# A diffusion layer on one Trainium2 core: the DRAM additions of the halves of `w_down` in quarters, one transfer to a channel of the up stage

## The chip, the cores and the metric

The kernel runs on one core of a Trainium2 chip. A core has five engines with a queue each: TensorE (PE) for matrix products, VectorE (DVE), ScalarE (ACT) and GpSimd (POOL) for work on elements, and SyncE (SP), which here only issues DMAs. The weight loads of PE are shown on their own as PEld. Sixteen DMA engines move data between DRAM and the on-chip memory, and from DRAM to DRAM. A DMA is issued by an instruction in some engine's queue: SP's and POOL's are the ones that matter here.

The metric is the device time of one execution in microseconds (us). The time before is 1707.95 us, the median of three runs (1703.12 to 1720.14).

## The reference

One layer of a bidirectional hybrid backbone: a mixer of two groups of gated linear recurrences (GLA and HGRN2), then a convolutional feed-forward block, both modulated by a conditioning vector. There are 128 context tokens and 1024 latent tokens (a grid of 16 rows of 64), and the model width is 1024. The change touches the feed-forward block alone:

```python
def conv_ffn(h, w_up, conv_w, conv_b, w_down, grid):
    u = dw_conv(h @ w_up, conv_w, conv_b, grid)     # w_up: 1024 x 5632; 3x3 depthwise conv
    gate, up = jnp.split(u, 2, axis=-1)             # 2816 hidden channels each
    return (jax.nn.silu(gate) * up) @ w_down        # w_down: 2816 x 1024

def trunk_layer(x, mod, ...):
    ...
    h = rmsnorm(x, norm2) * (1 + scale2) + shift2
    x = x + gate2 * conv_ffn(h, w_ffn_up, ffn_conv, b_ffn_conv, w_ffn_down, grid)
```

Everything is in float32. The outputs are the two token blocks after a last RMSNorm, and the new recurrence states of the context.

## The kernel before, in words

**Products.** A float32 operand is split into a high part (a copy in the matrix format, on ACT) and a low part (the difference, `split_lo`, L62, on POOL or DVE), and a product is three matrix products of such parts. The two large products of the feed-forward block are done with seven block products in place of eight, which needs sums of blocks of both operands.

**The up stage** is a loop over 22 channels (L1531); a channel is 128 gate columns and the 128 up columns that go with them. For each channel PE does seven products of 12 matrix multiplications each (`up`, L1457), the same columns for the 128 context tokens (`up_prompt`), and two transposes (`prompt_columns`, L1507). The transposes come once per channel and so mark PE's place. DVE and ACT do the convolutions out of PSUM (`conv_rows`, `conv_prompt`).

**The weights of a channel** come in two rows, row 1 for the gate columns and row 2 for the up columns. `load_row` (L1284) loads a row in two halves of 256 KB into the tile `ra`, issued by SP; each moves 512 runs of 512 bytes to 128 partitions. `weight_sums` (L1305) makes four block sums out of both rows on POOL: first s1 = row-2 block 1 + row-2 block 2 (L1307), then s2 (L1308), s4 (L1309) and s3 (L1310), in the tile `sr`. `split_slots` (L1292) makes the high and low parts for PE (`wuh` on ACT, `wul` on POOL). Rows are fetched ahead: in iteration c of the loop the rows of channel c+2 are loaded as soon as the splits and sums of channel c+1 have freed their part of `ra`. Row 2 is issued first; L1307 is the first instruction that needs it.

**The second half of a channel** (`second_half`, L1515) runs one iteration later: the rest of the convolution, the product of the gated halves on POOL (L1522), the store of the result to the DRAM tile `scr_g` (L1523, issued by POOL), one transfer out of `sums_todo` if any is left (channels 1 and up; issued by POOL right behind L1522), and in odd channels the sums over tokens (`token_sums`, L1384, four POOL instructions and a store to `scr_s`).

**The down stage** also uses seven products, over 11 pairs of channels, with the operands read back from DRAM. Four of its weight operands are sums of blocks of `w_down`; they are made in DRAM, in the four tiles `scr_t` of 11 x 128 x 512 floats (2,816 KB each), by the transfers of `sums_todo`. `halves[h][f]` is a view of `w_down`: 11 blocks of 128 rows that lie 256 rows apart, 512 of the 1024 columns. In `scr_t` the same 1,408 rows lie one behind the other. A transfer with `accum_op=ALU.add` adds its source to what the destination holds; the others copy. The eight transfers go out with channels 1 to 8. The sums are read in the third, fifth, sixth and seventh of the down stage's eight products. Its first weights are fetched by SP during the last channels, from `scr_g` and `w_down`.

**What sets the order.** PE's products of the up stage are chained by hand (`chained`, L1449); the rest is placed by a scheduler at build time, in each engine's one in-order queue. The transfers of `sums_todo` are tied to follow L1522 of their channel. POOL's DMAs all go through one queue (q0 in the profile), SP's through another (q1).

Of the kernel before, what the change touches and what calls it, by code (L numbers as in the profile page):

```python
# [13 lines left out]
ALU = mybir.AluOpType  # L14
# [11 lines left out]
NPAIR = 11  # L26
# [20 lines left out]
def kernel(ctx: ExitStack, tc: tile.TileContext, ins, outs, stop=None):  # L47
    nc = tc.nc
# [40 lines left out]
    scr_t = [dram.tile([NPAIR, P, 512], F32, name=f"scr_t{i}") for i in range(4)]  # L89
# [1294 lines left out]
    def token_sums(j):  # L1384
# [8 lines left out]
        nc.gpsimd.dma_start(scr_s[j], t)  # L1393


    halves = [
        [w_down.rearrange("(j h p) f -> h j p f", h=2, p=P)[h][:, :, fs] for fs in (lo_f, hi_f)] for h in range(2)
    ]
    sums_todo = [
        lambda: nc.gpsimd.dma_start(scr_t[0], halves[0][1]),  # L1400
        lambda: nc.gpsimd.dma_start(scr_t[2], halves[1][1]),
        lambda: nc.gpsimd.dma_start(scr_t[0], halves[0][0], accum_op=ALU.add),
        lambda: nc.gpsimd.dma_start(scr_t[2], halves[0][1], accum_op=ALU.add),
        lambda: nc.gpsimd.dma_start(scr_t[1], scr_t[0]),
        lambda: nc.gpsimd.dma_start(scr_t[1], halves[1][1], accum_op=ALU.add),
        lambda: nc.gpsimd.dma_start(scr_t[3], scr_t[1]),
        lambda: nc.gpsimd.dma_start(scr_t[3], halves[1][0], accum_op=ALU.add),
    ]

    def conv_rows(u, ch, acc, ra=0, rb=NROW):  # L1410

# [393 lines left out]
def build(nc, shapes, outs_kind="ExternalOutput", stop=None):  # L1805
    ins = {
        n: nc.dram_tensor(f"in_{n}_dram", s, dt, kind="ExternalInput").ap() for n, (s, dt) in shapes.items()
    }
    outs = [
        nc.dram_tensor(f"out_{i}_dram", s, F32, kind="ExternalOutput").ap() for i, (s, _) in enumerate(_OUTS)  # L1810
    ]
    with tile.TileContext(nc, schedule_with_timeline_sim=True) as tc:
        kernel(tc, ins, outs, stop)
# [14 lines left out]
```

## Time and profile before

| | |
|---|---|
| median of three runs | 1707.95 us (1703.12 to 1720.14) |
| profiled execution: its own time | 1704.19 us |
| its span, first to last instruction | 1702.4 us |
| granted clock of PE over the span | 0.972 |
| PE busy | 1599.4 us (94%) |
| DVE busy | 1189.7 us (70%) |
| ACT busy | 752.5 us (44%) |
| POOL busy | 712.5 us (42%) |
| up stage, first to last transposes of PE | 921 to 1438 us |
| down stage | from about 1440 us to the end |

Busy times are shares of the whole span and say nothing of a single stage. In the lists quoted below, a row of a timeline has the start in us, the duration in us, the engine, the line, the operation, output and input by the program's names; in brackets the idle time of the engine just before it and what ended it. A row of DMA issues has the number of issues, the size of one, and the median time from issue to landing. A row of stretches has the stretch, its length, then for each engine the busy time and the count of instructions, the granted clock, the mean busy share of the 16 DMA engines, and GB/s read and written together.

### The profile page before, as it was taken

What the parts mean: (1) busy time and instruction counts of PE and PEld (TensorE: products, weight loads), DVE (VectorE), ACT (ScalarE), POOL (GpSimd) and SP (SyncE); (2) the same over time, 40 slices, a digit from 0 to 9 for tenths busy, and PEclk for the clock granted to TensorE, in tenths of its full rate; (3) what the DMA queues carried; (4) which work ended last, traced back from release to release, by engine and by line L of the source; (5) the groups of instructions that cost most, each with busy time, mean ns of one, the idle gap of its engine ahead of it and who ended that gap; (6) DMA issues with size and microseconds to landing.
All of it is one profiled execution on the core that took longest, in us unless ns stands there. A gap on an engine that the chain in (4) does not pass through costs nothing.

```text
span 1702.4 us, 23982 instructions
## 1 busy us (share of the span) xinstructions
PE 1599.4 (94%) x9050; PEld 1346.1 (79%) x9050; DVE 1189.7 (70%) x1720; ACT 752.5 (44%) x1397; POOL 712.5 (42%) x523
## 2 busy tenths in 40 slices
PE   7999998999999999899877998789999999999997
PEld 2788886998999999878656887567788887788886
DVE  4554456066576667854669997678899999777665
ACT  4443345253545344511664443333444444447444
POOL 2402012232423323111255987777999997300001
PEclk9999999999999999999978999899899999999999
DMA  9234343221322304253821357676222224679862
GB/s 353 78 95 124 116 132 106 74 90 50 111 64 69 115 32 157 77 230 139 306 99 38 115 183 170 190 188 157 98 94 102 96 97 147 253 259 338 284 193 117
DMA packets 166349, 244.18 MB, mean 143 GB/s; under 512 B 14132, under 2 KB 110626, under 8 KB 164186
## 3 DMA queue, kind: packets, MB, share of 16 engines
q1 hardware_dynamic: 142583, 168.54, 30.8%
q0 software_dynamic: 23040, 73.43, 13.1%
q8 instruction: 71, 1.16, 0.3%
q10 hardware_dynamic: 611, 0.68, 0.1%
q14 instruction: 44, 0.36, 0.1%
HBM read 186.95 MB, written 78.71 MB: 156 GB/s over the span
## 4 chain that ended last, share of the span: by engine, by line
PE 73%; DMA 9%; POOL 6%; DVE 6%; issue 4%; ACT 1%; SPq 0%; POOLq 0%; DVEq 0%; ACTq 0%
PE u L1316 16%; PE mm L580 15%; PE mm L594 6%; PE lv L862 5%; PE xb L1690 5%; PE yb L1690 5%; DMA ra<-in_w_ffn_up_dram 5%; PE mm L720 3%; PE x L1490 3%; POOL wul L62 2%; PE yb L1741 2%; PE u L1211 2%; PE mm L485 1%; PE x L903 1%; PE o L938 1%
## 5 line engine op out<-in xcount | busy, mean ns | idle before, releaser
L1426 DVE SCALAR_TENSOR_TENSOR acc<-u,convc,acc 128x945 f32<-128x945 f32 (+2 forms) x352 | 426.8, 1218 | 10.8 <-ACT acc L1414 4.4
L62 POOL TENSOR_TENSOR wl<-raw,wh 128x1024 fp32r<-128x1024 f32 x42 | 102.1, 2435 | 271.8 <-ACT wh L123 246.9
L580 PE MATMUL mm<-h1h,wh 128*128 128x384 f32 x528 | 184.7, 350 | 0.0
L580 PE MATMUL mm<-h1l,wh 128*128 128x384 f32 x528 | 180.9, 343 | 0.0
L580 PE MATMUL mm<-h1h,wl 128*128 128x384 f32 x528 | 180.9, 343 | 0.0
L862 PE MATMUL lv<-Q,m 64*128 64x128 f32 (+1 forms) x1008 | 126.6, 295 | 12.5 <-DVE Q L871 6.7
L879 DVE COPY_PREDICATED S<-masks,lv 128x384 f32<-128x384 uint8 x168 | 98.7, 587 | 54.5 <-PE lv L862 54.3
L62 POOL TENSOR_TENSOR wul<-sr,wuh 128x512 fp32r<-128x512 f32 (+1 forms) x68 | 121.9, 1793 | 33.5 <-ACT wuh L1302 33.1
L855 ACT ACTIVATE m<-k 128x384 f32<-128x384 f32 x126 | 69.8, 556 | 142.3 <-DVE k L873 119.2
L871 DVE TENSOR_TENSOR Q<-Q,fb 128x384 f32<-128x384 f32 x126 | 92.8, 736 | 54.7 <-PE lv L862 54.0
L862 PEld LDWEIGHTS lv<-Q,m 64*128 64x128 f32 (+1 forms) x1008 | 107.5, 190 | 26.6 <-issue 10.7
L62 POOL TENSOR_TENSOR wul<-ra,wuh 128x1024 fp32r<-128x1024 f32 x46 | 116.6, 2535 | 11.8 <-ACT wuh L1302 7.6
L580 PEld LDWEIGHTS mm<-h1h,wh 128*128 128x128 f32 x528 | 100.3, 190 | 5.5 <-issue 3.7
L580 PEld LDWEIGHTS mm<-h1l,wh 128*128 128x128 f32 x528 | 100.1, 190 | 1.5 <-issue 0.8
L1665 POOL TENSOR_TENSOR sq<-sq,mhalf 128x1 f32<-128x1 f32 x9 | 11.1, 1237 | 214.1 <-DVE sq L1662 214.1
L580 PEld LDWEIGHTS mm<-h1h,wl 128*128 128x128 f32 x528 | 99.9, 189 | 0.7 <-issue 0.6
L123 ACT ACTIVATE wh<-raw 128x1024 fp32r<-128x1024 f32 x55 | 58.1, 1058 | 62.3 <-DMA raw<-in_w_in_dram 22.8
L594 PE MATMUL mm<-wh,h1h 128*128 128x256 f32 x288 | 83.2, 289 | 0.0
L594 PE MATMUL mm<-wl,h1h 128*128 128x256 f32 x288 | 80.9, 281 | 0.0
L873 DVE TENSOR_TENSOR k<-k,fb 128x384 f32<-128x384 f32 x126 | 76.1, 608 | 6.7 <-ACT m L855 2.7
L594 PE MATMUL mm<-wh,h1l 128*128 128x256 f32 x288 | 80.8, 281 | 0.0
L1302 ACT ACTIVATE wuh<-ra 128x1024 fp32r<-128x1024 f32 x44 | 46.3, 1053 | 62.0 <-DMA ra<-in_w_ffn_up_dram 27.4
(346 smaller groups left out, 4478.9 us busy)
## 6 DMA issues: line engine op xcount, KB each, us to landing
ra<-in_w_ffn_up_dram SPq DMA_DIRECT2D x88, 256.0 KB, 3.1
scr_t<-in_w_ffn_down_dram POOLq DMA_DIRECT2D x6, 2816.0 KB, 27.0
raw<-in_w_in_dram SPq DMA_DIRECT2D x32, 512.0 KB, 4.5
raw<-in_w_ada_dram SPq DMA_DIRECT2D x32, 512.0 KB, 3.7
scr_g<-acc POOLq DMA_DIRECT2D x22, 576.0 KB, 4.0
scr_s<-late POOLq DMA_DIRECT2D x11, 1024.0 KB, 5.0
wa<-in_w_ada_dram SPq DMA_DIRECT2D x16, 512.0 KB, 6.1
raw<-in_w_out_dram SPq DMA_DIRECT2D x13, 512.0 KB, 10.0
```

What stands on the lines that cost most here:

```text
L62: eng.tensor_tensor(out, full, hi.bitcast(F32), op=ALU.subtract)
L123: nc.scalar.activation(hi, raw, AF.Copy)
L580: mm(ps, a[:, kt, :], h[kt][b], start=(n == 0), stop=(n == 23))
L594: mm(ps, h[kt][t // 3][:, ts_], a[:, kt % 4, :], start=(n == 0), stop=(n == 23))
L855: nc.scalar.activation(aps(kmix, 0, [[2 * h, NB], [h, 2], [1, h]]), aps(kf_, 0, [[2 * h, NB], [BL + h, 2], [1, h]]), AF.Copy)
L862: last = mm(ps[:, i, :], kmix[r0:r1, i * P : (i + 1) * P], aps(Qf_, i * P, dims, r0, r1), start=True, stop=True,)
L871: nc.vector.tensor_tensor(qm, qm, aps(ff_, 2 * h - 1, [[BL - h, 2], [2 * h, NB], [0, h]]), op=ALU.mult)
L873: nc.vector.tensor_tensor(km, km, aps(ff_, BL + 2 * h - 1, [[-(BL + h), 2], [2 * h, NB], [0, h]]), op=ALU.mult)
L879: nc.vector.copy_predicated(S_, masks[:, lev : lev + 1, :].to_broadcast([P, 3, P]), ps)
L1316: last = mm(dst, W[x][:, a, kt, :], HB[y][b][:, kt, :], start=(start and n == 0), stop=(stop and n == 11), skip_group_check=True,)
L1426: last = nc.vector.scalar_tensor_tensor(o, u3[:, r0 + dy : r1 + dy, c0 + dx : c1 + dx], wc(3 * (dy + 1) + dx + 1), o, op0=ALU.mult, op1=AL ...
L1690: anchor["down"] = mm(banks[i], w[a][:, ts_], w[b][:, 512:1024], start=(start and j == 0 and n == 0), stop=(j == NPAIR - 1 and n == 2), sk ...
```

## The change

The four additions are cut along the 11 blocks into pieces of 3, 3, 3 and 2. The four copies stay whole. `sums_todo` grows from 8 to 20 entries, one of which goes out with each channel from 1 to 20, in the same order of tiles as before.

```diff
-    sums_todo = [
-        lambda: nc.gpsimd.dma_start(scr_t[0], halves[0][1]),
-        lambda: nc.gpsimd.dma_start(scr_t[2], halves[1][1]),
-        lambda: nc.gpsimd.dma_start(scr_t[0], halves[0][0], accum_op=ALU.add),
-        lambda: nc.gpsimd.dma_start(scr_t[2], halves[0][1], accum_op=ALU.add),
-        lambda: nc.gpsimd.dma_start(scr_t[1], scr_t[0]),
-        lambda: nc.gpsimd.dma_start(scr_t[1], halves[1][1], accum_op=ALU.add),
-        lambda: nc.gpsimd.dma_start(scr_t[3], scr_t[1]),
-        lambda: nc.gpsimd.dma_start(scr_t[3], halves[1][0], accum_op=ALU.add),
-    ]
+    sums_todo = []
+
+    def sum_copy(i, src):
+        sums_todo.append(lambda: nc.gpsimd.dma_start(scr_t[i], src))
+
+    def sum_add(i, src):
+        for j in range(0, NPAIR, 3):
+            js = slice(j, min(j + 3, NPAIR))
+            sums_todo.append(lambda js=js: nc.gpsimd.dma_start(scr_t[i][js], src[js], accum_op=ALU.add))
+
+    sum_copy(0, halves[0][1])
+    sum_copy(2, halves[1][1])
+    sum_add(0, halves[0][0])
+    sum_add(2, halves[0][1])
+    sum_copy(1, scr_t[0])
+    sum_add(1, halves[1][1])
+    sum_copy(3, scr_t[1])
+    sum_add(3, halves[1][0])
```

So the additions go out with channels 3 to 6 (tile 0), 7 to 10 (tile 2), 12 to 15 (tile 1) and 17 to 20 (tile 3), and the copies with channels 1, 2, 11 and 16.

## The prediction

> **What bounds the kernel now.** I read the page first, then the busy time by stretch, then who waits for whom, then POOL's timeline.
>
> ```profile
> span 1702.4 us, 23982 instructions
> ...
> POOL 2402012232423323111255987777999997300001
> ...
> DMA  9234343221322304253821357676222224679862
> ```
>
> The span is cut into 40 slices of 42.6 us. The up stage is slices 22 to 33: POOL is busy nearly throughout, and DMA stands at 5 to 7 in the first half of it and at 2 in the second. That is where the transfers into `scr_t` run, one per channel, in channels 1 to 8. The same stage by stretch, each stretch one channel (columns: length, busy time per engine, granted clock, DMA share, GB/s):
>
> ```profile
> core 0: us, PE busy (x) PEld busy (x) DVE busy (x) ACT busy (x) POOL busy (x), PEclk, DMA share, GB/s
> 1046.20:1078.80 32.60, 24.42 (x110) 19.81 (x110) 21.82 (x23) 9.03 (x13) 20.99 (x14) 0.87 0.70 151
> 1134.80:1157.80 23.00, 19.95 (x85) 16.09 (x85) 16.75 (x18) 8.56 (x12) 22.62 (x18) 0.85 0.65 219
> 1157.80:1190.20 32.40, 28.91 (x138) 23.42 (x136) 26.96 (x29) 12.46 (x17) 20.97 (x14) 0.99 0.73 158
> 1235.30:1258.00 22.70, 22.70 (x112) 18.65 (x111) 21.93 (x24) 10.46 (x14) 22.28 (x17) 1.00 0.33 119
> 1258.00:1280.60 22.60, 22.60 (x112) 18.64 (x111) 21.75 (x24) 10.46 (x14) 19.13 (x14) 1.00 0.22 73
> ```
>
> An undisturbed channel takes 22.65 us (the last two rows, halved) and PE fills it. A channel with an addition (first and third row) takes over 32 us and no engine fills it. A channel with a copy `scr_t`<-`scr_t` (second row) takes 23.0. What the additions make late, from the waits between 940 and 1200 us (us in total, times, longest):
>
> ```profile
> POOL sr L1307 <- DMA ra<-in_w_ffn_up_dram: 47.2, 6, 11.9
> ...
> PE u L1316 <- POOL wul L62: 21.3, 4, 8.2
> ```
>
> POOL waits for the next channel's row-2 weights, and PE then waits for POOL's splits. POOL's own timeline shows the loop:
>
> ```profile
> 1012.94 2.69 POOL L1522 TENSOR_TENSOR acc<-acc,acc 128x1152 f32<-128x1152 f32 x1
> 1015.58 1.91 POOL L1402 DMA_DIRECT2D scr_t<-in_w_ffn_down_dram  x1
> 1016.76 2.06 POOL L62 TENSOR_TENSOR wul<-sr,wuh 128x512 fp32r<-128x512 f32 x1
> ...
> 1042.10 1.27 POOL L1307 TENSOR_TENSOR sr<-ra 128x512 f32<-128x512 f32 x1 [9.25 <-DMA ra<-in_w_ffn_up_dram]
> ...
> 1046.22 2.66 POOL L1522 TENSOR_TENSOR acc<-acc,acc 128x1152 f32<-128x1152 f32 x1
> ...
> 1078.82 2.64 POOL L1522 TENSOR_TENSOR acc<-acc,acc 128x1152 f32<-128x1152 f32 x1
> 1081.40 0.56 POOL L1404 DMA_DIRECT2D scr_t<-scr_t  x1
> 1081.96 1.29 POOL L62 TENSOR_TENSOR wul<-sr,wuh 128x512 fp32r<-128x512 f32 x1
> ...
> 1101.91 2.69 POOL L1522 TENSOR_TENSOR acc<-acc,acc 128x1152 f32<-128x1152 f32 x1
> ...
> 1134.78 2.64 POOL L1522 TENSOR_TENSOR acc<-acc,acc 128x1152 f32<-128x1152 f32 x1
> ...
> 1157.76 2.70 POOL L1522 TENSOR_TENSOR acc<-acc,acc 128x1152 f32<-128x1152 f32 x1
> ...
> 1190.23 2.64 POOL L1522 TENSOR_TENSOR acc<-acc,acc 128x1152 f32<-128x1152 f32 x1
> ```
>
> From one L1522 to the next the four channels with an addition take 33.28 (1012.94 to 1046.22), 32.60, 32.87 (1101.91 to 1134.78) and 32.47 us (1157.76 to 1190.23): 32.81 on the mean, 10.15 over 22.65, 40.6 in all. So the question is what an addition of a quarter does to the row-2 load that follows it.
>
> **The change part by part.** *The pieces.* Two copies from `w_down` stay in channels 1 and 2. The four additions become sixteen, of 3, 3, 3 and 2 of the 11 blocks (768 and 512 KB), in channels 3 to 10, 12 to 15 and 17 to 20; the copies `scr_t`<-`scr_t` move to channels 11 and 16. On PE, DVE, ACT and SP the built program's order is unchanged; POOL gets twelve more DMAs and a few neighbouring swaps among L1309, L1310, L62 and L1393. The bytes are unchanged.
>
> *How long a quarter occupies the engines it uses.* No row shows a quarter. These are the transfers of 2,816 KB (last number: us to landing), the SP issue of the load behind an addition, and the DMA share while one transfer is nearly alone:
>
> ```profile
> scr_t<-in_w_ffn_down_dram POOLq DMA_DIRECT2D x1, 2816.0 KB, 14.4
> ...
> scr_t<-in_w_ffn_down_dram POOLq DMA_DIRECT2D x1, 2816.0 KB, 27.4
> ...
> scr_t<-scr_t POOLq DMA_DIRECT2D x1, 2816.0 KB, 12.7
> ...
> 1025.53 0.37 SPq L1287 DMA_DIRECT2D ra<-in_w_ffn_up_dram  x1
> ...
> 970.40:971.20 0.80, 0.80 (x5) 0.66 (x4) 0.77 (x2) 0.80 (x2) 0.80 (x2) 1.00 0.72 257
> ...
> 1036.00:1039.00 3.00, 3.00 (x14) 2.41 (x13) 2.96 (x4) 0.00 (x0) 0.00 (x0) 1.00 0.77 145
> ...
> 1086.00:1088.00 2.00, 1.96 (x7) 1.58 (x8) 1.97 (x2) 1.17 (x1) 2.00 (x3) 0.79 1.10 360
> ```
>
> By proportion a quarter takes 27.4 x 3/11 = 7.5 us: the lower end. The upper end is no shortening at all, 27.4. Two rows decide. The copy from `w_down` keeps 0.72 of 16 engines busy (970.40), the addition 0.77 with load packets among it (1036.00); the copy whose outermost dimension has 64 rows keeps all busy (1086.00: 1.10, as packets of two queues overlap). 11/16 is 0.69, and the outermost dimension of `w_down`'s view is the 11 blocks. I read that as one engine per block: 11 engines with 128 rows, 256 KB, each. A quarter has 3 blocks, the last one 2: then 3 or 2 engines, again with 128 rows each. 768/3 = 512/2 = 256 KB, so **a quarter takes as long as the whole, 27 us**, on fewer engines. I take the upper end.
>
> [...]
>
> *What the load meets.* The row-2 load goes to 128 partitions; I assume that it needs every engine, as it lands late even though 5 engines carry no addition. Its second half is issued at 1025.53 and POOL starts on it at 1042.10, 16.5 us later. It needs the slowest engine alone, so three loaded engines hold it as eleven do. The addition begins before the load in both kernels (issue 1015.58) and outlasts it, so the wait is that of before.
>
> *Cost of a channel with a quarter.* POOL's slot for the DMA was 1.18 us (1015.58 to 1016.76) with 1,408 rows and 0.56 (1081.40 to 1081.96) with 64; 384 rows give some 0.7 in between, 0.45 less. It stands on the loop, as POOL does not wait between L1522 and the load's issue. Period 32.81 - 0.45 = 32.35, or 9.7 over 22.65. If the slot does not shrink: 10.15.
>
> *How often.* A quarter in channel c is issued while the loop prepares row 2 of channel c+3, and the last row is that of channel 21. So the quarters of channels 3 to 10, 12 to 15, 17 and 18 meet a load: 14. Those of 19 and 20 meet none. The sum: 14 x 9.7 = 135.8 added, 4 x 10.15 = 40.6 removed, **+95**. The moved copies keep their price (1078.82 to 1101.91 is 23.09, 0.4 over). New waits on POOL: the quarters of 12 and 17 and the copy of 16 wait for the transfer one channel earlier, which has landed (27.4 us of 32, 12.7 of 23), so they cost nothing.
>
> *The start of the down stage.* The quarter of channel 20 runs past the end of the channel loop, and the store of `scr_g` for that channel stands behind it in the same queue. SP's in-order queue waits for that store:
>
> ```profile
> 1437.99 2.67 POOL L1522 TENSOR_TENSOR acc<-acc,acc 128x1152 f32<-128x1152 f32 x1 [0.54 <-DVE acc L1426]
> ...
> 1451.03 2.67 SPq L120 DMA_DIRECT2D raw<-scr_g  x2
> ...
> 1480.57 1.06 ACT L123 ACTIVATE wuh<-raw 128x1024 fp32r<-128x1024 f32 x1 [0.45 <-DMA raw<-in_w_ffn_down_dram]
> ...
> 1481.53 2.04 ACT L1622 ACTIVATE gate<-yb 128x512 f32<-128x512 f32 x4
> ```
>
> The quarter would be issued at 1437.99 + 2.6 and land 27 us later, near 1468 on this clock; the load at 1451 moves there, 17 us. Most of that is covered: ACT waits for a later load until 1480.57 anyway, and the gate copies on which PE's next product waits come at 1481.53. The moved load and its splits are done some 7 us before that, but more loads stand behind it in SP's queue. Bounds: 0 and +17; I take +3, nearer to the covered end.
>
> **Sum:** 1704.2 + 95 + 3 = **1802 us**. 1704.2 is the profiled execution's own time; the median of the runs shown is 1707.95, 3.8 above it, so a median may read a little higher too.
>
> **The rivals.** *Proportional pieces (faster).* If all sixteen engines, or eleven, carry a quarter, it lands some 8 us after its issue. The load was issued 10 us after the addition's (1015.58 to 1025.53) and would meet an empty queue; a copy of 12.7 us at this place costs 0.4, so it decides below some 12 us. POOL's slots of 0.7 would vanish in its idle time (22.28 and 19.13 busy of 45.3 in two channels). For the gain, PE's transposes, one pair per channel:
>
> ```profile
> 1034.42 0.38 PE L1507 MATMUL x<-ident,late 128*128 128x128 f32 x2
> ...
> 1214.23 0.38 PE L1507 MATMUL x<-ident,late 128*128 128x128 f32 x2
> 1236.89 0.38 PE L1507 MATMUL x<-ident,late 128*128 128x128 f32 x2
> ```
>
> Six channels took 179.8 us where six of 22.66 take 136.0: 43.8 to gain, so 1661 us with 1 left at the down stage. For it: equal bytes at equal rate is the plain expectation. Against it: the 0.72. [...]
>
> *Few engines, but quicker rows.* With 3 engines at work the memory is less loaded. If each wait is 1.7 us shorter (a tenth of 16.5), 14 x 1.7 = 24 go: 1778. Against: the copy at 257 GB/s (970.40) and the addition at 145 (1036.00) hold nearly the same share, so the engine rather than the memory seems to set the pace.
>
> *More waits behind the queue.* The stores of `scr_g` and `scr_s` stand behind each quarter, and the down stage may pay its full 17: 1816, or 1830 with one more us in each of 14 channels.
>
> *The change does not do what it says.* Twenty transfers, one to a channel from 1 to 20, are in the program; I give this nothing.
>
> **How the numbers follow.** Few engines with the waits of before 0.62, quicker rows 0.14, more waits 0.13: all slower. Proportional 0.09. A mixture that ends near 1704 has 0.02. The range takes the three slow cases and a little more, 1772 to 1832. The runs of before lie within 1% (1703.12 to 1720.14), about what a measurement can tell from no change, so the limits are 1691 and 1725. Faster 0.09, same 0.02, slower 0.89.
>
> **What would show it.** A quarter of 768 KB landing after 25 us or more, and the one of 512 KB too; L1307 waiting 7 to 12 us in fourteen channels and not four; L1522 every 32 us from channel 3 to 10; PE under 0.8 busy over most of the up stage. I am wrong if quarters land within 10 us and L1307 does not wait.

## The result, and the profile after

| | before | after |
|---|---|---|
| median | 1706.68 us (1703.12 to 1720.14, 4 runs) | 1805.36 us (1802.91 to 1814.28, 4 runs) |
| profiled execution: its own time | 1704.19 us | 1802.91 us |
| its span | 1702.4 us | 1801.1 us |
| granted clock of PE over the span | 0.972 | 0.942 |

The changed kernel is slower: 1.0572 times the time before, 95% interval 1.0504 to 1.0641. The lines after the diff have moved by 9: L1522 is now L1531, L1523 is L1532; an addition is issued in L1408, a copy in L1403.

The page of the profile after, the same three rows as were shown of before:

```profile
span 1801.1 us, 24010 instructions
...
POOL 2401111232423231112569957768775878400001
...
DMA  9133350231413231648213533334433445579863
```

A slice is now 45 us, and the up stage ends in slice 34. POOL is at 5 to 8 from slice 23 to 33, also at the end of the stage, where it stood at 9 before: the holes now reach over the whole of it. DMA stands at 3 to 5 in the same slices, where the channels with additions had 5 to 7 before: the engines as a whole are less busy, though more is late.

Stretches of the kernel after, from one L1531 to the next (length, busy time per engine, granted clock, DMA share, GB/s); the first, second and fourth have a quarter, the third a copy:

```profile
1051.23:1082.89 31.66, 24.37 (x110) 19.72 (x110) 21.13 (x22) 9.02 (x12) 20.95 (x14) 0.88 0.34 79
1082.89:1116.08 33.19, 27.66 (x110) 21.76 (x110) 22.35 (x25) 12.12 (x16) 23.86 (x18) 0.81 0.39 104
1278.09:1300.81 22.72, 20.13 (x82) 16.15 (x83) 16.46 (x17) 8.57 (x11) 22.59 (x17) 0.81 0.72 246
1300.81:1332.93 32.12, 29.31 (x140) 23.73 (x138) 27.34 (x30) 12.47 (x17) 21.09 (x15) 1.00 0.33 76
```

A channel with a whole addition took 32.60 and 32.40 us in these columns before, with a DMA share of 0.70 and 0.73. A channel with a quarter takes the same time with half the share: fewer engines are held, for as long. The channel with the copy takes 22.72, as an undisturbed one did. PE's lower granted clock (0.88 in the first row, 0.942 over the span) doesn't set the length: in that channel POOL's 20.95 us of work and its one wait for the load, 10.71 us in the timeline below, already are the 31.66.

What waits for what between 940 and 1560 us, kernel after (us in total, times, longest):

```profile
POOL sr L1307 <- DMA ra<-in_w_ffn_up_dram: 132.4, 15, 11.5
...
PE u L1316 <- POOL wul L62: 65.6, 13, 8.0
```

Before it was 47.2 us in 6 waits and 21.3 in 4: the same pair of waits at the same length, by PE's count 13 times in place of 4. POOL's timeline of the kernel after (start, duration, in brackets the idle time before and what ended it):

```profile
1017.87 2.69 POOL L1531 TENSOR_TENSOR acc<-acc,acc 128x1152 f32<-128x1152 f32 x1
1020.49 1.95 POOL L1408 DMA_DIRECT2D scr_t<-in_w_ffn_down_dram  x1
1021.67 2.11 POOL L62 TENSOR_TENSOR wul<-sr,wuh 128x512 fp32r<-128x512 f32 x1
...
1047.70 1.25 POOL L1307 TENSOR_TENSOR sr<-ra 128x512 f32<-128x512 f32 x1 [9.20 <-DMA ra<-in_w_ffn_up_dram]
...
1051.23 2.64 POOL L1531 TENSOR_TENSOR acc<-acc,acc 128x1152 f32<-128x1152 f32 x1
...
1079.38 1.27 POOL L1307 TENSOR_TENSOR sr<-ra 128x512 f32<-128x512 f32 x1 [10.71 <-DMA ra<-in_w_ffn_up_dram]
...
1118.67 1.97 POOL L1408 DMA_DIRECT2D scr_t<-in_w_ffn_down_dram  x1
...
1144.36 1.26 POOL L1307 TENSOR_TENSOR sr<-ra 128x512 f32<-128x512 f32 x1 [10.84 <-DMA ra<-in_w_ffn_up_dram]
...
1450.94 2.71 POOL L1531 TENSOR_TENSOR acc<-acc,acc 128x1152 f32<-128x1152 f32 x1
...
1480.71 1.26 POOL L1307 TENSOR_TENSOR sr<-ra 128x512 f32<-128x512 f32 x1 [9.11 <-DMA ra<-in_w_ffn_up_dram]
...
1484.24 2.65 POOL L1531 TENSOR_TENSOR acc<-acc,acc 128x1152 f32<-128x1152 f32 x1
...
1503.27 3.36 POOL L1531 TENSOR_TENSOR acc<-acc,acc 128x1152 f32<-128x1152 f32 x1
```

The first L1531 is that of channel 3, the last two are those of channels 18 and 19. The quarter issued at 1118.67 is the first one of 512 KB, and the wait behind it is no shorter than behind one of 768 KB. Between two L1531 channel 17 (from 1450.94) takes 33.30 us; channel 18 (from 1484.24) takes 19.03, although it has a quarter too. Thirteen channels are stalled, 3 to 10, 12 to 15 and 17, by 32.56 us on the mean (31.66 to 33.36).

The DMA issues of the kernel after (size of one, median us to landing): the first row is a single quarter of 768 KB, the second a single one of 512 KB, the last two all loads of `ra` and all stores of `scr_g`:

```profile
scr_t<-in_w_ffn_down_dram POOLq DMA_DIRECT2D x1, 768.0 KB, 26.8
...
scr_t<-in_w_ffn_down_dram POOLq DMA_DIRECT2D x1, 512.0 KB, 27.1
...
ra<-in_w_ffn_up_dram SPq DMA_DIRECT2D x88, 256.0 KB, 10.3
...
scr_g<-acc POOLq DMA_DIRECT2D x22, 576.0 KB, 24.8
```

Before, a whole addition of 2,816 KB landed after 27.4. A load of `ra` landed after 3.1 at the median, and a store of `scr_g` after 4.0.

**Where the 98.7 us of span come from**, measured at POOL's L1531 (L1522 before). The way to that of channel 1, where nothing is changed, took 4.55 us more (969.34 against 964.79); over the kernels run it varies from 963.4 to 975.8, so I take this for scatter and not the change. Channel 1 to 3: +0.4. Channel 3 to 18: 466.37 us against 381.05, **+85.3**. Channel 18 to 21: 71.95 against 66.97, +5.0. Channel 21 to the end: 244.91 against 241.44, +3.5. The sum is 98.75.

For the experiments below I therefore also give **the rest**, the span minus the start of L1531 of channel 1. It was 737.6 us before and is 831.8 after.

### The profile page after: what moved, and what is told of

Read it like the earlier page. It is cut to its first block, busy times and chain, and to the rows that moved or that the text cites. A ratio compares the mean times of both kernels' runs of the same rounds, so it can differ in the third digit from the quotient of the medians.

```text
span 1801.1 us, 24010 instructions
## 1 busy us (share of the span) xinstructions
PE 1634.5 (91%) x9050; PEld 1369.6 (76%) x9050; DVE 1186.7 (66%) x1720; ACT 753.6 (42%) x1397; POOL 732.5 (41%) x535
## 3 DMA queue, kind: packets, MB, share of 16 engines
q1 hardware_dynamic: 142583, 168.54, 29.1%
q0 software_dynamic: 47808, 73.63, 13.1%
HBM read 186.95 MB, written 78.71 MB: 147 GB/s over the span
## 4 chain that ended last, share of the span: by engine, by line
PE 56%; DMA 19%; POOL 13%; issue 5%; DVE 4%; ACT 2%; SPq 0%; POOLq 0%; ACTq 0%; DVEq 0%
PE mm L580 14%; DMA ra<-in_w_ffn_up_dram 12%; POOL wul L62 6%; PE mm L594 6%; PE xb L1699 5%; PE lv L862 5%; PE yb L1699 5%; PE u L1316 4%; PE mm L720 3%; DMA scr_g<-acc 3%; PE yb L1750 2%; PE u L1211 2%; PE o L938 1%; PE x L903 1%; PE mm L485 1%
## 5 line engine op out<-in xcount | busy, mean ns | idle before, releaser
L62 POOL TENSOR_TENSOR wul<-sr,wuh 128x512 fp32r<-128x512 f32 (+1 forms) x68 | 134.1, 1973 | 14.6 <-ACT wuh L1302 14.3
L62 POOL TENSOR_TENSOR wul<-ra,wuh 128x1024 fp32r<-128x1024 f32 x46 | 126.2, 2745 | 15.1 <-ACT wuh L1302 7.9
L862 PEld LDWEIGHTS lv<-Q,m 64*128 64x128 f32 (+1 forms) x1008 | 108.1, 192 | 26.8 <-issue 11.0
L1316 PE MATMUL u<-b22h,wul 128*128 128x512 f32 x88 | 47.3, 537 | 65.6 <-POOL wul L62 65.6
L1452 DVE SCALAR_TENSOR_TENSOR acc<-x,convc,acc 128x127 f32<-128x127 f32 x88 | 30.3, 344 | 106.8 <-ACT acc L1448 106.8
L1307 POOL TENSOR_TENSOR sr<-ra 128x512 f32<-128x512 f32 x22 | 29.1, 1323 | 133.1 <-DMA ra<-in_w_ffn_up_dram 132.4
## 6 DMA issues: line engine op xcount, KB each, us to landing
scr_g<-acc POOLq DMA_DIRECT2D x22, 576.0 KB, 24.8
```

The costliest lines, as they stand in the source:

```text
L62: eng.tensor_tensor(out, full, hi.bitcast(F32), op=ALU.subtract)
L862: last = mm(ps[:, i, :], kmix[r0:r1, i * P : (i + 1) * P], aps(Qf_, i * P, dims, r0, r1), start=True, stop=True,)
L1316: last = mm(dst, W[x][:, a, kt, :], HB[y][b][:, kt, :], start=(start and n == 0), stop=(stop and n == 11), skip_group_check=True,)
```

## The experiments

**Theory**, from the 0.72 of 16 engines that 11 blocks kept busy and from the 27 us that 11, 3 and 2 blocks all took: an addition occupies as many engines as its outermost dimension has rows, 16 at most, for a time that the rows on one engine set; the row-2 load waits for the engine that is held longest. **Rivals:** the load is held up by the share of the engines or of the memory that is taken; or by something else in the lopsided spread; or by the adding. A run that has one time and no range is a single execution, of a kernel that leaves part of the sums out; its rest is compared, as what lies ahead of channel 1 scatters.

### The same quarters, written so that 128 rows are outermost

```diff
-            sums_todo.append(lambda js=js: nc.gpsimd.dma_start(scr_t[i][js], src[js], accum_op=ALU.add))
+            d_, s_ = (t[js].rearrange("j p f -> p j f") for t in (scr_t[i], src))
+            sums_todo.append(lambda d_=d_, s_=s_: nc.gpsimd.dma_start(d_, s_, accum_op=ALU.add))
```

> The quarters of the change, the same bytes in the same channels, but with source and destination written row first (128 rows, then 3 or 2 blocks) in place of block first. Nothing is left out. Theory (the outermost dimension sets the number of engines, and the row-2 load waits for the slowest engine): 128 rows spread over all 16 engines, 24 rows on each in place of 128. A quarter lands in 7 to 9 us in place of 27, the row-2 load is issued behind it, L1307 waits in no channel after 2, PE's transposes come every 22.7 us, and the time is 1660 us (1653 to 1670), below both kernels. Rival 1 (a DRAM addition holds the queue some 27 us whatever its spread): 27 us and 1800. Rival 2 (half of it: the addition is limited by the memory, not by the engine): landing 12 to 18 us and 1690 to 1750.

Measured: 1665.74 us (1660.4 to 1668.2), 0.9718 times before (0.9683 to 0.9754; before had 1713.42 on that chip). The rest is 694.9 us. The page and the waits of this kernel:

```profile
ra<-in_w_ffn_up_dram SPq DMA_DIRECT2D x88, 256.0 KB, 3.0
...
scr_t<-in_w_ffn_down_dram POOLq DMA_DIRECT2D x12, 768.0 KB, 8.1
...
POOL sr L1307 <- DMA ra<-in_w_ffn_up_dram: 3.4, 2, 2.8
```

The same bytes, the same twenty transfers in the same channels, added in the same way: only the order of the dimensions differs. A quarter lands after 8.1 us in place of 27, `ra` after 3.0, and no L1307 behind a quarter waits; the two waits left come behind the copies of channels 1 and 2. This kernel beats both others, and the prediction's first rival had the price about right: it gave 1661 us for quarters that land in some 8 us.

### The whole additions, 128 rows outermost

```diff
-        for j in range(0, NPAIR, 3):
-            js = slice(j, min(j + 3, NPAIR))
+        for j in range(0, NPAIR, NPAIR):
+            js = slice(j, NPAIR)
```

with the row order of the kernel above.

> The four additions whole, as before the change and in channels 3, 4, 6 and 8, but written row first (128 rows, then 11 blocks). Nothing is left out. Theory: 16 engines with 88 rows each in place of 11 with 128. The addition starts 2.6 us after its issue; when the row-2 load comes, 8.7 us after the issue, 39 rows are done and 49 are left; load packets and rows alternate at 0.19 us per pair for those 49, then the load is free. It lands some 9 us after its second half's issue in place of 16.4, the four channels take 25 to 26 us in place of 32.8, and the time is 1675 us (1666 to 1685). Rival (size and not spread counts): landing 27 us, 1704. The addition itself lands after 18 to 20 us by the theory.

Measured: 1688.76 us (1686.93 to 1691.93), 0.9863 times before (0.9824 to 0.9902); the rest is 721.4 us.

```profile
POOL sr L1307 <- DMA ra<-in_w_ffn_up_dram: 27.9, 5, 7.5
```

The landing was as expected, 19.8 us. The waits were not: L1307 waited 5.3 to 7.5 us behind each of the four additions, so that these channels took 28.3 to 29.5 us, and the time came out above the range. The waits still follow the landing (19.8 against 27.4, 5 to 7 against 9 to 12), but the load comes 2 us or more later than the addition's own landing says. The packets of channel 3 show what is left to do in between. By 1034, when the addition issued at 1014.34 had its last rows on the way (it landed after 20.4 us), SP's queue had moved 576 packets, and row 2 alone has 1,024; from 1034 to 1036 it moved 792 more. In the same 2 us POOL's queue moved 93 packets with 0.34 MB. At 3.7 KB on the mean, where a row of the addition has 2 KB and one of the store of `scr_g` right behind it 4.5, most of them are by estimate of that store.

So spreading over 16 engines is worth part of the gain, and cutting into quarters the rest: 0.986 with the first alone, 0.972 with both, 1.057 with the second alone.

### The quarters copied, not added

```diff
-            sums_todo.append(lambda js=js: nc.gpsimd.dma_start(scr_t[i][js], src[js], accum_op=ALU.add))
+            sums_todo.append(lambda js=js: nc.gpsimd.dma_start(scr_t[i][js], src[js]))
```

> The change as it is, except that the sixteen quarters copy in place of adding; the sums of the weight blocks are left out, so the last product's operands are other numbers. Block first, so still 3 or 2 engines. Theory (what counts is how long the few engines stay busy): 64 packets of two rows at 0.16 us, landing 13 to 15 us like the whole copy's 14.4; L1307 waits 0 to 3 us as after channels 1 and 2; the time is 1661 to 1690. Rival (any transfer on few engines holds the load, for the packets it puts between): waits of 7 us and more, 1760 to 1800.

Measured: 1675.05 us, landing 14.1, waits of L1307 24.2 us in 10 (3.6 at most); the rest is 708.3 us. On the same engines a copied quarter took half of what an added one took (27.0), and what a whole copy took (14.4 us in the profile before). For a quarter the long stall needed both, few engines and the double time of an addition: L1307 waited up to 11.5 us with both, 2.8 with the additions on 16 engines, 3.6 with copies on few. (A whole addition still stalled on all 16, by up to 7.5 us.)

### Without the last two quarters

```diff
+    del sums_todo[18:]
```

> The change as it is without the quarters of channels 19 and 20; the sum for the last 5 of the 11 pairs of the fourth tile is left out. Theory: these two meet no row-2 load, but the store of the hidden channel stands behind them and SP waits for it at the start of the down stage; without them the stretch from L1531 of channel 18 to the end of the span is 4 to 9 us shorter than in the changed kernel (316.9 us there), and the time is about 1796. Rival (the late quarters are covered by the convolution and its splits): that stretch is the same within 1 us, 1803.

Measured: 1795.04 us; from channel 18 to the end 308.35 us, against 316.86 with them. They cost 8.5 us in all: 4.3 from channel 18 to 21 and 4.2 behind that, against the prediction's 3. This is one profile of each; between the changed kernel and the last one below, which has transfers of the same length in these channels, the same stretch differs by 2.6 us (319.48 there). L1307 waits 134.3 us in 16, as with them, so no load of row 2 meets these two.

### One block to a quarter

```diff
-            js = slice(j, min(j + 3, NPAIR))
+            js = slice(j, j + 1)
```

> Each of the sixteen additions takes one block (256 KB) in place of three or two; 24 + 4 of the 44 blocks are so left out of the sums. Theory (one engine per block with 128 rows of 2 KB, and the row-2 load waits for its slowest engine): one engine alone then has the same 128 rows as three had, the addition lands after 25 to 28 us, L1307 waits 8 to 12 us in the same 13 channels, and the time is that of the changed kernel, 1790 to 1806 us. Rival (the load is held up by how much of the engines or of the memory is taken): a third of the bytes gives a third of the wait, 2 to 4 us in each of 13 channels, and 1690 to 1725 us.

Measured: 1660.34 us, one wait of L1307 (0.5 us), the rest 694.9 us. Neither theory's number. One of these additions, by the list of DMA issues:

```profile
scr_t<-in_w_ffn_down_dram POOLq DMA_DIRECT2D x1, 256.0 KB, 4.7
```

It landed in 4.7 us, the first one in 3.9: this was not one engine with 128 rows. By 1018 the first one has 144 packets, 128 with a row and 16 under 512 B. 134 of them start in the 2 us from 1016 and take 72.6% of the time of 16 engines, where 11 engines have 69% at most. With a single block the outermost dimension with more than one entry is that of the 128 rows; I read the run as these rows spread over all 16 engines, as in the first experiment. It says nothing on what a load waits for. On the spread it says, together with the 256 KB in two half blocks below, which landed after 13.8 us, that the transfer's size didn't decide it.

### Quarters cut along the columns

```diff
-        for j in range(0, NPAIR, 3):
-            js = slice(j, min(j + 3, NPAIR))
-            sums_todo.append(lambda js=js: nc.gpsimd.dma_start(scr_t[i][js], src[js], accum_op=ALU.add))
+        for k in range(4):
+            ks = slice(128 * k, 128 * (k + 1))
+            sums_todo.append(lambda ks=ks: nc.gpsimd.dma_start(scr_t[i][:, :, ks], src[:, :, ks], accum_op=ALU.add))
```

> The quarters are cut along the 512 columns: 11 blocks x 128 rows x 128 columns, 704 KB each, in place of 3 blocks x 128 rows x 512 columns. Theory (an engine per block, the time by the bytes that the busiest engine has): 11 engines with 64 KB each in place of 256 KB, landing after 7 to 9 us, no wait of L1307 behind a quarter, 1655 to 1672 us. Rival (an engine takes its time per row, whatever its length): 128 rows per engine as before, now of 512 bytes, landing near 27 us, waits as in the changed kernel, 1790 to 1806 us. If a row of 512 bytes costs half of one of 2 KB: 13 to 15 us and 1661 to 1690 us, as where the quarters were copied.

Measured: 1675.45 us (1667.53 to 1680.47), 0.9795 times before (0.9751 to 0.9838; before had 1711.08 on that chip). A quarter landed after 12.6 us, and L1307 waited 6.3 us in 6. That is close to the third case, a row of 512 bytes at about half the time of one of 2 KB: 128 rows per engine in 12.6 us in place of 27, just under the 13 to 15 foretold. Neither bytes alone nor rows alone set the time.

### 127 rows of one block, and 61

```diff
-            js = slice(j, min(j + 3, NPAIR))
-            sums_todo.append(lambda js=js: nc.gpsimd.dma_start(scr_t[i][js], src[js], accum_op=ALU.add))
+            js = j
+            sums_todo.append(lambda js=js: nc.gpsimd.dma_start(scr_t[i][js, 0:127], src[js, 0:127], accum_op=ALU.add))
```

> As the run with one block, but 127 of its 128 rows (254 KB), so that the outermost dimension is 127, which no count from 2 to 16 divides; the other rows and blocks are left out of the sums. [...] Rival A (rows are dealt over 16 engines evenly, or nearly so): landing near 5 us, no waits, 1655 to 1665 us. [...]

Measured: 1660.72 us, landing 4.5, L1307 waiting 2.7 us in 2, the rest 695.3 us: rival A. The 127 rows landed as the 128 of one block did (3.9 to 4.7), far from the 26.9 of 128 rows on an engine in the run with two blocks below.

The second kernel has `0:61` in place of `0:127`.

> As the run with 127 rows, with 61 (122 KB; 61 is prime as well), the rest left out of the sums. [...]

Measured: 1672.45 us, landing 3.1, L1307 waiting 3.2 us in 2, the rest 694.8 us; the difference to the 127 rows lies ahead of channel 1. By landing and packets the 61 rows too were dealt over 16 engines, 4 to each, so no engine was held for long and this run says nothing on what a load waits for. That the rows were dealt is read from the count of packets:

```profile
DMA packets 160397, 236.79 MB, mean 143 GB/s; under 512 B 11780, under 2 KB 108274, under 8 KB 158234
```

That is the kernel with 127 rows. The kernel of the first experiment has 11,765 packets under 512 B; this one has 15 more and the one with 61 rows (11,812) 47 more: one and three for each of the sixteen additions, within one packet. 127 + 1 = 16 x 8 and 61 + 3 = 16 x 4. By these counts an addition of 61 rows has 61 packets with a row and 19 under 512 B, 3 more than the 16 of one block with 128 rows. That fits 8 or 4 rows to each of 16 engines, with a packet under 512 B for each row that is missing; this is a reading of the counts, and whether the rows are dealt one by one or in runs, they can't tell.

### Two blocks: half of the rows, and all

```diff
-            js = slice(j, min(j + 3, NPAIR))
-            sums_todo.append(lambda js=js: nc.gpsimd.dma_start(scr_t[i][js], src[js], accum_op=ALU.add))
+            js = slice(j, j + 2)
+            sums_todo.append(lambda js=js: nc.gpsimd.dma_start(scr_t[i][js, 0:64], src[js, 0:64], accum_op=ALU.add))
```

> Each addition takes two blocks, and of each its first 64 rows (256 KB in all); the rest is left out of the sums. Theory (one engine per block, 0.2 us for a row of 2 KB, the row-2 load waits for the engine that is held longest): two engines with 64 rows each, landing after 12 to 14 us, waits of L1307 of 0 to 3 us, 1655 to 1690 us; under 512 B there are 11,764 + 16 x 14 x 64 = 26,100 packets. Rival (it is the lopsided spread or the empty packets that hold the load up, not the time of the longest engine): waits of 5 us or more, 1720 us or more.

Measured: 1677.02 us, L1307 waiting 18.2 us in 8 (3.7 at most), the rest 708.2 us. A single one of these additions, by the DMA issues, and the packets:

```profile
scr_t<-in_w_ffn_down_dram POOLq DMA_DIRECT2D x1, 256.0 KB, 13.8
...
DMA packets 174734, 236.93 MB, mean 141 GB/s; under 512 B 26101, under 2 KB 122595, under 8 KB 172571
```

The second kernel has `scr_t[i][js], src[js]`, all 128 rows.

> As the run with two half blocks, with all 128 rows of both blocks (512 KB); the other blocks are left out of the sums. Theory: two engines with 128 rows each, landing after 25 to 28 us, waits of L1307 of 8 to 12 us in 13 channels, 1785 to 1812 us, as in the changed kernel, though 14 of 16 engines carry nothing of the addition; 11,764 + 16 x 14 x 128 = 40,436 packets under 512 B. Rival (the load is held up by the share of the engines or of the memory that is taken): two thirds of the wait, 6 to 7 us, and 1745 to 1765 us.

Measured: 1805.7 us, the rest 834.8 us (831.8 in the changed kernel). The page and the waits:

```profile
scr_t<-in_w_ffn_down_dram POOLq DMA_DIRECT2D x16, 512.0 KB, 26.9
...
DMA packets 191117, 241.24 MB, mean 134 GB/s; under 512 B 40436, under 2 KB 136930, under 8 KB 188954
...
POOL sr L1307 <- DMA ra<-in_w_ffn_up_dram: 133.3, 16, 11.5
```

This pair settles what the run with one block had left open. With two engines of sixteen held, and two thirds of the bytes, the load waits as long as behind three engines or eleven: 133.3 us against 132.4. With the same two engines held half as long nearly all of it goes: 18.2 us. What counted in these runs, up to the 128 rows on an engine that were tried, is how long the engine that is held longest is held, 13.8 or 26.9 us by the landing. The share of the engines and the lopsided spread by itself are out.

## Why the prediction was right, point by point

It was right: 1802 us foretold, 1802.91 in the profiled execution and 1805.36 at the median, by the likeliest case. The mechanism was right too; not every term was, and that the sum came within 1 us is luck.

**The pieces and the engines: right.** "A quarter takes as long as the whole, 27 us": 26.8 and 27.1 for 3 and 2 blocks. The row orders show that the outermost dimension is the reason (8.1 us for 768 KB with 128 rows outermost), and the packets show the count. Of before and after:

```profile
DMA packets 166349, 244.18 MB, mean 143 GB/s; under 512 B 14132, under 2 KB 110626, under 8 KB 164186
```

```profile
DMA packets 191117, 244.37 MB, mean 136 GB/s; under 512 B 38900, under 2 KB 135394, under 8 KB 188954
```

The bytes read and written in DRAM are the same on both pages (186.95 and 78.71 MB). There are 24,768 more packets, all under 512 B, and the 0.19 MB more that the rows count are some 8 bytes for each; I call them empty. If an engine without a block gets 128 empty packets for each transfer, a transfer of 3 blocks has 13 x 128 of them, of 2 blocks 14 x 128, of 11 blocks 5 x 128. Twelve quarters of 3, four of 2 and four whole additions less make 128 x (156 + 56 - 20) = 24,576, and 12 more transfers with 16 each, as one block's addition has them beside its rows, 192. That is 24,768. The four whole additions with 128 rows outermost agree: that kernel has 11,572 packets under 512 B, 2,560 fewer than before, which is 4 x 5 x 128. So the reading of 0.72 as 11 engines holds. What sets the count of engines for shapes that were not tried, no run here shows.

One reading beside it was wrong, without effect. The share of 1.10 at 1086.00 is not two queues that overlap: all packets that start in that stretch are of POOL's queue, 16 with 0.72 MB, 45 KB each. That makes 64 of them in 2,816 KB, as the prediction has it. 1.10 times the 2 us on 16 engines are 2.2 us for each of the 16, longer than the stretch; by estimate such a packet is counted whole where it starts.

**What the load meets: right, and now shown.** The assumption that the load waits for its slowest engine was the one with least under it; the pair with two blocks bears it out. How the load is held up can be read from the packets of POOL's queue (q0) and SP's (q1), from 1035 to 1039 in the kernel after and from 1036 to 1039 in the one before:

```profile
q0 software_dynamic: 61, 0.12, 16.8%
q1 hardware_dynamic: 61, 0.03, 3.9%
...
q0 software_dynamic: 170, 0.35, 62.3%
q1 hardware_dynamic: 168, 0.09, 14.3%
```

For each row of the addition (2 KB) one packet of the load (512 bytes) goes through, behind three engines as behind eleven. 61 rows in 4 us on 3 engines are 5 a us on each. Row 2 has 1,024 packets, 64 for each of 16 engines if they are spread evenly, so by estimate it needs some 13 us as long as rows are left, however many engines have them. It does not have to wait for the addition's end: the quarter issued at 1118.67 landed 27.1 us later, at 1145.77, and L1307 behind it started at 1144.36. A still longer addition need not make the load later, then; no run has more than 128 rows on an engine.

**Cost of a channel: the slot was mis-sized.** POOL's slot for a quarter was to shrink from 1.18 to 0.7 us. It is 1.18 (1020.49 to 1021.67). In the run with 128 rows outermost it is 0.85 for the same 768 KB (1019.10 to 1019.95), so it is not the rows with data alone that set it. The prediction's own fallback, 10.15 for each stall, was nearer to the measured 9.91 than the 9.7 it took. Over 13 stalls that is +2.7.

**How often: the count was wrong by one.** Of the 14 stalls, the one of channel 18 did not come. "A quarter in channel c is issued while the loop prepares row 2 of channel c+3" was off by one: the last wait, at 1480.71, ends the period of channel 17, and channel 18 takes 19.03 us with no L1307 left to wait. The load behind channel c's quarter is that of channel c+4, and 21 - 4 is 17. That is -9.7.

**The start of the down stage: the term was too small, as a place was missing.** The stretch behind L1531 of channel 21 lost 3.5 us, near the 3 foretold. But 5.0 were lost ahead of it, in channels 18 to 20, for which the prediction had no term. The timeline of after, POOL, ACT and SP:

```profile
1508.30 2.09 POOL L1532 DMA_DIRECT2D scr_g<-acc  x1
...
1535.73 1.36 POOL L1532 DMA_DIRECT2D scr_g<-acc  x1
...
1537.45 0.46 ACT L1448 ACTIVATE acc<-x,vcol,convc 128x128 f32<-128x128 f32 x1 [5.67 <-DMA scr_g<-acc]
...
1547.09 0.33 SPq L120 DMA_DIRECT2D raw<-in_w_ffn_down_dram  x1
1564.59 0.80 SPq L120 DMA_DIRECT2D raw<-scr_g  x2
...
1567.29 1.06 ACT L123 ACTIVATE wuh<-raw 128x1024 fp32r<-128x1024 f32 x1 [8.06 <-DMA raw<-scr_g]
```

SP stands for 17 us until the store of `scr_g` behind the last quarter is done, as foretold, and the cover over it held. The missing place is the row of L1448: a convolution needs an accumulator that a store of `scr_g` still reads. The store of channel 19 was issued at 1508.30 behind the quarter of its channel and lands 29.1 us later, when ACT goes on. ACT waits 5.67 us for it, which is about the loss, and without the last two quarters no instruction waits for a store of `scr_g` there (1500 to 1560). That this wait is the whole of it is argued; that the last two quarters cost 8.5 us is measured.

**The sum.** Foretold +98 (+95 and +3), measured +98.7 of span. It holds to 1 us because the errors cancel: one stall too many (-9.7) against +2.7 of longer stalls, +5.5 at the end and +4.55 of scatter ahead of channel 1. These make +3.05; what is left, -2.3, lies in channels without a stall, which differ by that much (channel 16 takes 20.36 us after, 22.28 before).

**The rivals.** Proportional pieces was the right mechanism for a kernel that spreads its rows (8.1 us for a quarter), which this one does not. Quicker rows: no, 27 us on 2, 3 and 11 engines. More waits behind the queue: the stores land late (24.8 us), at a price of about 5 us.

## What to carry to other kernels

Before cutting a DRAM transfer into pieces, look at what the cut does to its outermost dimension: an addition of few outer rows kept few engines here, for as long as the whole did, and the row-2 load was as late (the longest wait of L1307 was 11.5 us, 11.9 before). Try the order with the longest dimension outermost; here that alone turned a loss of 5.7% into a gain of 2.8% with the same bytes in the same places. The DMA share was no measure of how late a load would be: 0.34 and 0.39 in the channels with a quarter, 0.70 and 0.73 in those with a whole addition, with the same stall.

## What the runs showed of the hardware that was not expected

**The rows on the busiest engine gave the landing of an addition, over the sizes that were run.** Additions with rows of 2 KB; the engines and the rows on one are worked out from the shapes and the counts of packets above:

| rows on the busiest engine | transfer | landing, us |
|---|---|---|
| 4 | 122 KB on 16 engines | 3.1 |
| 8 | 256 KB on 16 | 3.9 to 4.7 |
| 16 | 512 KB on 16 | 5.9 |
| 24 | 768 KB on 16 | 8.1 |
| 64 | 256 KB on 2 | 13.8 |
| 88 | 2,816 KB on 16 | 19.8 |
| 128 | 512 KB on 2, 768 KB on 3, 2,816 KB on 11 | 26.9, 27.0, 27.4 |

By an estimate made on these, 2.3 us and 0.19 us a row, all of them come out within 1.3 us. 256 KB took 3.9 to 4.7 us as one block of 128 rows and 13.8 as two of 64.

**By the counts, engines without data get packets all the same.** In an addition they are as many as the rows of a block: 128 for each idle engine and transfer, 64 where the blocks have 64 rows (26,101 packets under 512 B, 26,100 foretold), 40,436 with two whole blocks, as foretold to the packet. Where the quarters were copied the page has 25,332, which is 64 for each idle engine although the blocks have 128 rows: the copy has two rows in a packet, by the estimate in the next paragraph. They took next to no time: POOL's queue has 23,040 packets before and 47,808 after, and on both pages all of them together take 13.1% of the 16 engines' span. By estimate from that, on spans of 1702.4 and 1801.1 us, the 24,768 more took no more than 10 ns each. The count of packets under 512 B on the page thus told, in these kernels, how many engines a transfer uses.

**An addition took twice the time of a copy** on the same engines, 27.0 against 14.1 us for the quarters. From 970.40 to 971.20 in the kernel before, in a whole copy, POOL's queue moved 160 packets with 0.21 MB in 71.8% of the 16 engines' time; 110 of them are under 512 B, so the other 50 have by estimate 4 KB, two rows, and took at most 0.18 us each. In the addition, from 1036.00 to 1039.00, its 170 packets have 2 KB, one row, and took 0.18 us each as well.
